# The low parts of every fourth weight chunk by an accumulating DMA, in a two-layer encoder in fp32

## The chip, the core and the metric

The kernel runs on one core of a Trainium2 chip. The engines that matter here are TensorE (matrix products), VectorE and ScalarE (elementwise work), GpSimd (hardly used before) and SyncE, from whose queue most transfers are issued. In the profile they are called PE (PEld for its weight loads), DVE, ACT, POOL and SP; a "q" behind the name is the engine's instruction queue where it issues a DMA. The metric is the device time of the whole kernel in microseconds.

## What is computed

The reference is an encoder of two layers on 256 tokens of width 2048, all in fp32. Each layer has a mixer (an mLSTM group, a retention group and a multi-head latent attention group, whose outputs are joined) and a feed-forward block:

```python
for l in range(DEPTH):                                   # DEPTH = 2
    h = _rms(x, g_mix[l])
    x = x + _mixer(h, cos, sin, w_in[l], ..., w_out[l])
    u = _rms(x, g_ffn[l])
    x = x + jnp.square(jax.nn.relu(u @ w_ff1[l])) @ w_ff2[l]     # 2048 -> 8192 -> 2048
return _rms(x, g_final)
```

Nearly all the arithmetic is products of the 256 tokens with weights: w_in (2048 x 4432), w_out (2048 x 2048), w_ff1 and w_ff2 (2048 x 8192 each way), and the smaller up-projections of the attention group.

## The kernel before

**Three products for one.** TensorE takes operands in a format (fp32r) that carries fewer bits than fp32 and goes through the array in one pass. The kernel therefore splits each operand into a high part, which is the value rounded to that format, and a low part, which is the rest. A product of two fp32 matrices becomes high x high, high x low and low x high.

**The stream of weights.** All weights lie in one flat array in the order of their use, cut into 737 chunks of 128 partitions x up to 1024 columns (512 KB). `weight_plan` writes that order down. The class `Stream` carries it out:

- `load` issues the DMA of a chunk from SyncE's queue into a tile `wraw`. There are NRAW = 4 buffers.
- `prep` makes the parts of a chunk: ScalarE copies `wraw` into `whi` (line 237), which rounds it, and VectorE writes `wlo = wraw - whi` (line 238). Then it asks for the load of the chunk four further on, for which a raw buffer must be free.
- `get(i)`, called when the products of chunk i are put down, first calls `prep` up to chunk i + 2. There are NHL = 4 buffers each of `whi` and `wlo`.

**The order of work.** The program is written straight out, and each engine executes its own list in that order; semaphores order the engines among each other. So the split of chunk i stands on ScalarE's list at the point where the products of chunk i - 2 begin, behind everything that was put down before that point. In the feed-forward part this matters: the blocks alternate between ff1 (four chunks, two tiles of hidden units, `ff_tile`) and ff2 (four chunks, one block of 512 output columns, `nat`). When a hidden tile is complete, `ff_evac` squares its positive part and splits it, with ScalarE's copy `fr` (line 1051), two VectorE operations, ScalarE's `hhi` (line 322) and VectorE's `hlo`. ScalarE's `fr` waits until TensorE has finished the tile. The first chunk split behind the second tile's evacuation is the third chunk of the ff2 block that follows.

**Which chunks the number falls on.** Chunks 0 to 112 of layer 0 are the mixer's; from 113 on the blocks of the feed-forward part begin at an index with remainder 1 when divided by 4. Layer 1 begins at chunk 369 and its feed-forward part at 481, again with remainder 1. So in the feed-forward parts the chunks with i % 4 == 3 are the third chunks of their blocks (for the very first ff1 block, the chunks are ordered otherwise, the third of the four as well). Of the 64 ff2 blocks of the two layers 56 follow an ff1 block and 8 follow another ff2 block.

**SyncE's queue** is in order: a load that waits for a raw buffer holds up every load behind it.

Of the kernel before, what the change touches and what calls it, by code (L numbers as in the profile page):

```python
# [18 lines left out]
P = 128  # L19
# [15 lines left out]

# columns of the constant array
C_MASK = 0
# [3 lines left out]
C_W = 816  # L41
# columns of a layer's parameter array
G_MIX, G_FFN, G_ML, G_RET, G_Q, G_KV, W_CONV, B_GATE, PAR_W = 0, 16, 32, 36, 40, 44, 46, 70, 86


# [1 line left out]
def weight_plan():  # L47
    """Blocks of weights in the order of their use; each is cut into chunks (k rows of tiles, columns)."""
    plan = []

    def nat(key, l, mat, kts, c0, w):
        per = max(1, CH // w)
        if not plan:
            kts0, kts = kts[:2], kts[2:]
            chunks = [([k], c0, w) for k in kts0]
        else:
            chunks = []
        chunks += [(kts[i:i + per], c0, w) for i in range(0, len(kts), per)]
        plan.append((key, l, mat, chunks))

    def stat(key, l, mat, kts, tiles):
        """One chunk per group of (tile, k) pairs, tile major."""
        per = CH // P
        pairs = [(t, k) for t in tiles for k in kts]
        chunks = [pairs[i:i + per] for i in range(0, len(pairs), per)]
        plan.append((key, l, mat, chunks))

    k16 = list(range(16))
    kout = [8, 9, 10, 11, 12, 13, 14, 15, 0, 1, 2, 3, 4, 5, 6, 7]
    for l in range(DEPTH):  # L70
        nat("c_q", l, "w_in", k16, 1024, 512)
        nat("c_kv", l, "w_in", k16, 1536, 336)
        nat("r_qk", l, "w_in", k16, 1872, 512)
        for h in range(0, 8, 4):
            stat(("kn", h), l, "w_kv_up", [0, 1], [h, h + 1, h + 2, h + 3])
        for b in range(2):
            nat(("v", b), l, "w_kv_up", [0, 1], 1024 + 512 * b, 512)
        for h in range(0, 8, 2):
            stat(("qn", h), l, "w_q_up", [0, 1, 2, 3], [h, h + 1])
        nat("qr", l, "w_q_up", [0, 1, 2, 3], 1024, 512)  # L80
        stat("ml_q", l, "w_in", k16, [0, 1, 2, 3])
        stat("ml_k", l, "w_in", k16, [4, 5, 6, 7])
        nat("ml_v", l, "w_in", k16, 2384, 512)
        nat("r_v", l, "w_in", k16, 2896, 512)
        nat("ml_o", l, "w_in", k16, 3408, 512)
        nat("r_g", l, "w_in", k16, 3920, 512)
        for part, kk in (("a", kout[:8]), ("b", kout[8:])):
            for b in range(2):
                nat(("out" + part, b), l, "w_out", kk, 512 * b, 512)
        for b in range(2, 4):  # L90
            nat(("out", b), l, "w_out", kout, 512 * b, 512)

        def ff1(g, i):
            f = g * 8 + 2 * i
            if g == 0 and i == 0:
                for half in range(2):
                    for t in range(2):
                        stat(("ff1", f + t, half), l, "w_ff1", k16[8 * half:8 * half + 8], [f + t])
            else:
                stat(("ff1", f), l, "w_ff1", k16, [f, f + 1])  # L100

        def ff2(g, b):
            nat(("ff2", g, b), l, "w_ff2", [g * 8 + i for i in range(8)], 512 * b, 512)

        for i in range(4):
            ff1(0, i)
        for g in range(NGRP):
            for i in range(4):
                if g + 1 < NGRP:
                    ff1(g + 1, i)  # L110
                ff2(g, i)
    return plan
# [8 lines left out]
def in_columns():  # L121
    """The columns of w_in in the order in which the blocks read them."""
    r = np.arange
# [85 lines left out]
class Stream:  # L209
    """The weights, chunk after chunk: read, then split into two parts that one pass carries exactly."""  # L210

# [17 lines left out]
    def prep(self, upto):  # L229
        while self.nprep < min(upto, len(self.sizes)):  # L230
# [6 lines left out]
            self.nc.scalar.activation(hi[:, :f], raw[:, :f], AF.Copy)  # L237
            self.nc.vector.tensor_tensor(lo[:, :f], raw[:, :f], hi[:, :f].bitcast(F32), op=ALU.subtract)  # L238
            self.parts[i] = (hi, lo)
# [10 lines left out]
def encoder_kernel(ctx: ExitStack, tc: tile.TileContext, xin, posin, w, par, const, gfin, out, dump=None):  # L250
# [13 lines left out]

# [1 line left out]
    cst = one.tile([P, C_W], F32, name="cst")  # L266
# [22 lines left out]

    # the clock of the tensor engine rises with use: products of zeros until the data is there  # L290
    warm = sp.tile([P, 512], mybir.dt.bfloat16, name="warm", tag="junk", bufs=1)
# [4 lines left out]

# [1 line left out]
    def bank(name):  # L298
# [6 lines left out]
    def rsqrt(dst, src, n, scale):  # L305
        """dst = 1 / sqrt(src * scale + EPS) on [P, n] by Newton's iteration, in steps."""
        nt = sp.tile([P, 3, n], F32, name="nt", tag=f"nt{n}", bufs=2 if n == 2 else 1)
# [11 lines left out]
    def split(*items):  # L319
        """hi + lo = src (* g) of each item, both in the one-pass format."""  # L320
        for hi, lo, src, *g in items:
# [12 lines left out]

# [1 line left out]
    side = []  # L336
    now = [0.0]

    class Task:
        """Steps of side work; a step yields the time to leave before the next one."""  # L340

# [43 lines left out]

# [1 line left out]
    chunk_no = [0]  # L387

    def nat_steps(chunks, ps, lh, ll, base, first, last):
        """ps[t] += (lh + ll)[k].T @ weights for both tiles of tokens."""  # L390
        n = sum(len(c[0]) for c in chunks)
# [21 lines left out]
    def stat(chunks, kts, rh, rl, dst):  # L413
        """dst[tile] = weights.T @ (rh + rl) for one tile of weight columns after another."""
        for c in chunks:
# [25 lines left out]
    def make_xT(b, g0, l, wait):  # L441
        """Columns 512 b .. of x, transposed and times the gain; their sums of squares."""
        for pr in range(2):
# [27 lines left out]
    def new_xT(b, g0, l, square, wait=0.8):  # L471
        """Starts the transposes of block b; after the last, the scale of the tokens."""
        xt_task[b] = add(make_xT(b, g0, l, wait), [(xt_task[b - 1], 2)] if b else [])
# [45 lines left out]
    def rope(dst, src, t, n):  # L519
        """Rotates n heads of 64: src [P, n * 64], dst that or [P, n, 64], of tile t of the tokens."""  # L520
        t1 = sp.tile([P, 512], F32, name="rp1", tag="rp1", bufs=1)[:, :n * 64]
# [15 lines left out]
    def layer(l):  # L537
        g = prm[:, l, :]
        L = {}

# [1 line left out]
        def ev_cq(ps):  # L542
# [60 lines left out]

# [1 line left out]
        def qr_task():  # L605
            qr = L["qr"]
            qd = ap.tile([P, 2, 8, 2, 64], F32, name="qd", tag="hlo", bufs=2)
            for t in range(2):
# [3 lines left out]
                yield 1.2  # L612
            # of each head the first part on 64 partitions, the second on the other 64
            qrT = L["qrT"] = ap.tile([P, 8, S], F32R, name="qrT", tag="hhi", bufs=2)
# [49 lines left out]

# [1 line left out]
        def gate_task():  # L666
# [31 lines left out]

            # lf <= 0, so that the running sum is never above its last term
            for d in range(2):  # L700
# [38 lines left out]

# [1 line left out]
        def ev_qk(i, pr, ps):  # L741
# [24 lines left out]

# [1 line left out]
        def ev_mlv(ps):  # L768
# [8 lines left out]
        def ml_head(h):  # L777
# [4 lines left out]
            hb, hs = L["hy"][:, 0], L["hs"]  # L782
            # blocks (direction, keys, queries): F00 F01 B10 B11 B00 F11
            wt = sp.tile([P, 768], F32, name="wt", tag="pr")
# [56 lines left out]
        def head_out(src, stat_, gate, k0, g0):  # L841
            """Normalises the heads in src, gates them and puts them at rows k0 .. of y transposed."""
            yhi, ylo = y0()
# [17 lines left out]

# [1 line left out]
        def ev_rqk(ps):  # L863
# [69 lines left out]

# [1 line left out]
        it = iter([p for p in plan if p[1] == l])  # L935
# [102 lines left out]

# [1 line left out]
        hts = {}  # L1040

        def ff_evac(f, ps):
            """The square of the positive part of tile f, split."""
            gi, i = divmod(f, 8)
# [11 lines left out]
        def ff_tile(ps, chunk, first, last):  # L1056
            """ps = [hi.T x + lo.T x's first part | hi.T x's second part]."""
            hi, lo = ws.get(chunk_no[0])
# [55 lines left out]

# [1 line left out]
    fin = {}  # L1116
# [13 lines left out]
    def last_block(chunks, lh, ll):  # L1130
        """The last columns, one tile of tokens after the other, each followed by its norm."""
        parts = []
# [82 lines left out]
```

## Time and profile before

| | us |
|---|---|
| median of 2 runs | 2184.4 |
| lowest and highest run | 2184.02, 2184.79 |
| span of the profiled execution | 2183.1 |
| TensorE products of a weight chunk with hidden units or xT in ff1 (f <- xT, whi and wlo) | 712.0 + 552.1 busy |
| ScalarE busy | 1044.0 |
| VectorE busy | 1354.7 |
| GpSimd busy | 0.2 |

The profile is of one execution. Its span is the time from the first to the last instruction, and the runs' times are a little longer than that. Busy times of an engine's instructions overlap where they are pipelined; TensorE's above all, so its groups add up to more than its busy time. A row of the timeline gives the start, the duration, the engine, the line, the operation with the tiles that it writes and reads, a count of instructions run together, and in brackets the idle time before it with what ended it.

### The profile page before, as it was taken

The page shows a single profiled execution, that of the slowest core. Times are in us where ns is not written, and L with a number is a line of the kernel's source. Part 1 is how long each engine was busy: PE and PEld are TensorE (multiplying, and loading weights), DVE is VectorE, ACT ScalarE, POOL GpSimd, SP SyncE. Part 2 cuts the span into 40 slices and gives each one's busy share as a digit, 9 for nine tenths or more (in the row PEclk, how much of TensorE's full clock was granted, in tenths as well). Part 3 has the DMA queues.
Part 4 walks back from the last instruction along what each step waited for, and adds up shares of the span by engine and source line. Part 5 has one row for each costly group of instructions (what it writes and reads, how often), then busy time and mean ns, then how long its engine had stood idle before and what let it go on. Part 6 is the DMA issues. An engine that isn't in the chain of part 4 may idle for free.

```text
span 2183.1 us, 29259 instructions
## 1 busy us (share of the span) xinstructions
PE 2164.9 (99%) x11280; PEld 1840.8 (84%) x11280; DVE 1354.7 (62%) x2019; ACT 1044.0 (48%) x1530; POOL 0.2 (0%) x4
## 2 busy tenths in 40 slices
PE   8999999999999999999999999999999999999998
PEld 7898888888888888888888978888888888888887
DVE  5667565666565656566666575756656565656655
ACT  5645655444444444444556455545444444444444
POOL 0000000000000000000000000000000000000000
PEclk9999999999999999999999999999999999999999
DMA  7544555566555556565565354555555555656554
GB/s 217 186 135 134 165 163 186 172 193 197 188 194 191 194 186 200 181 201 180 189 181 173 118 165 133 167 190 183 196 189 194 188 197 184 202 178 207 175 204 162
DMA packets 111356, 395.20 MB, mean 181 GB/s; under 512 B 12904, under 2 KB 14056, under 8 KB 111088
## 3 DMA queue, kind: packets, MB, share of 16 engines
q1 hardware_dynamic: 109072, 389.90, 54.7%
q10 hardware_dynamic: 2144, 3.43, 0.5%
q8 instruction: 88, 1.44, 0.3%
q14 instruction: 52, 0.43, 0.1%
HBM read 391.17 MB, written 2.12 MB: 180 GB/s over the span
## 4 chain that ended last, share of the span: by engine, by line
PE 95%; DVE 2%; ACT 1%; DMA 1%; issue 1%; ACTq 0%; SPq 0%; DVEq 0%
PE pm L333 57%; PE f L333 33%; PE sc L333 1%; DMA wraw<-in_w_dram 1%; DVE wlo L238 1%; PE o L333 1%; ACT whi L237 1%; PE ry L333 1%; PE num L333 0%; PE xt L330 0%; PE pt L330 0%; PE st L333 0%; ACT junk L303 0%; PE rs L333 0%; DVE mqk L765 0%
## 5 line engine op out<-in xcount | busy, mean ns | idle before, releaser
L238 DVE TENSOR_TENSOR wlo<-wraw,whi 128x1024 fp32r<-128x1024 f32 (+2 forms) x737 | 875.1, 1217 | 275.9 <-ACT whi L237 274.3
L237 ACT ACTIVATE whi<-wraw 128x1024 fp32r<-128x1024 f32 (+2 forms) x737 | 749.9, 1048 | 333.0 <-PE pm L333 286.6
L333 PE MATMUL f<-xT,whi 128*128 128x512 f32 x2048 | 712.0, 392 | 0.0
L333 PE MATMUL f<-xT,wlo 128*128 128x256 f32 x2048 | 552.1, 280 | 0.0
L333 PEld LDWEIGHTS f<-xT,whi 128*128 128x128 f32 x2048 | 379.4, 188 | 77.0
L333 PE MATMUL pm<-wlo,hhi 128*128 128x512 f32 (+1 forms) x1040 | 401.6, 386 | 0.6 <-DVE wlo L238 0.6
L333 PE MATMUL pm<-whi,hhi 128*128 128x512 f32 (+1 forms) x1040 | 402.1, 387 | 0.0
L333 PE MATMUL pm<-whi,hlo 128*128 128x512 f32 (+1 forms) x1040 | 401.2, 386 | 0.0
L333 PEld LDWEIGHTS f<-xT,wlo 128*128 128x128 f32 x2048 | 385.0, 188 | 11.3 <-DVE wlo L238 0.8
L333 PE MATMUL pm<-whi,xT 128*128 128x512 f32 (+1 forms) x896 | 291.3, 394 | 2.4 <-ACT whi L237 1.4
L333 PEld LDWEIGHTS pm<-wlo,hhi 128*128 128x128 f32 x1040 | 195.4, 188 | 40.2 <-DVE wlo L238 1.0
L333 PEld LDWEIGHTS pm<-whi,hlo 128*128 128x128 f32 x1040 | 195.4, 188 | 39.7
L1051 ACT ACTIVATE fr<-f 128x256 f32<-128x256 f32 x128 | 49.1, 384 | 374.3 <-PE f L333 374.3
L333 PEld LDWEIGHTS pm<-whi,hhi 128*128 128x128 f32 x1040 | 195.4, 188 | 37.2
L333 PEld LDWEIGHTS pm<-whi,xT 128*128 128x128 f32 x896 | 167.2, 189 | 37.5 <-ACT whi L237 1.6
L1052 DVE TENSOR_TENSOR fr<-f,fr 128x256 f32<-128x256 f32 x128 | 54.3, 424 | 218.0 <-ACT fr L1051 218.0
L1024 DVE SCALAR_TENSOR_TENSOR xx<-pm,rs,xx 128x512 f32<-128x512 f32 x126 | 90.1, 751 | 144.3 <-PE pm L333 144.3
L333 PE MATMUL pm<-wlo,xT 128*128 128x512 f32 (+1 forms) x448 | 173.5, 387 | 2.4 <-DVE wlo L238 2.3
L322 ACT ACTIVATE hhi<-fq 128x256 fp32r<-128x256 f32 x128 | 53.5, 418 | 126.8 <-DVE fq L1053 126.8
L333 PE MATMUL pm<-whi,yhi 128*128 128x512 f32 x256 | 101.5, 397 | 0.0
L333 PEld LDWEIGHTS pm<-wlo,xT 128*128 128x128 f32 x448 | 84.9, 189 | 19.6 <-DVE wlo L238 4.9
L333 PE MATMUL pm<-whi,ylo 128*128 128x512 f32 x256 | 99.8, 390 | 0.0
(235 smaller groups left out, 1614.7 us busy)
## 6 DMA issues: line engine op xcount, KB each, us to landing
wraw<-in_w_dram SPq DMA_DIRECT2D x723, 512.0 KB, 4.2
wraw<-in_w_dram SPq DMA_DIRECT2D x10, 504.0 KB, 6.7
wt<-mx_rows ACTq DMA_DIRECT2D x8, 256.0 KB, 3.7
out_dram<-xx SPq DMA_DIRECT2D x8, 256.0 KB, 3.3
xx<-in_x_dram SPq DMA_DIRECT2D x3, 512.0 KB, 8.1
gf<-in_gfin_dram ACTq DMA_DIRECT2D x1, 1024.0 KB, 6.1
xx<-in_x_dram SPq DMA_DIRECT2D x2, 256.0 KB, 3.8
wraw<-in_w_dram SPq DMA_DIRECT2D x2, 256.0 KB, 4.5
```

What stands on the lines that cost most here:

```text
L237: self.nc.scalar.activation(hi[:, :f], raw[:, :f], AF.Copy)
L238: self.nc.vector.tensor_tensor(lo[:, :f], raw[:, :f], hi[:, :f].bitcast(F32), op=ALU.subtract)
L322: A.activation(hi, src, AF.Copy, **({"scale": g[0]} if g else {}))
L333: T.matmul(ps, lhsT=lhsT, rhs=rhs, start=start, stop=stop)
L1024: V.scalar_tensor_tensor(x[t][:, xs], ps[t], scale[:, t:t + 1], x[t][:, xs], op0=ALU.mult, op1=ALU.add)
L1051: A.activation(r, ps[:, S:], AF.Copy)
L1052: V.tensor_tensor(r, ps[:, :S], r, op=ALU.add)
```

## The change

For every chunk i with i % 4 == 3 the subtraction on VectorE is left out. ScalarE makes the negative of the high part in the tile of the low part, by a second copy of the raw chunk with a scale of -1 (its output has the same rounded format), and a DMA issued from GpSimd's queue adds the raw chunk into that tile. The sum in the tile is the low part. The other chunks are as they were. Comments and docstrings of the file are dropped as well.

```diff
             self.nc.scalar.activation(hi[:, :f], raw[:, :f], AF.Copy)
-            self.nc.vector.tensor_tensor(lo[:, :f], raw[:, :f], hi[:, :f].bitcast(F32), op=ALU.subtract)
+            if i % 4 == 3:
+                self.nc.scalar.activation(lo[:, :f], raw[:, :f], AF.Copy, scale=-1.0)
+                self.nc.gpsimd.dma_start(out=lo[:, :f], in_=raw[:, :f], accum_op=ALU.add)
+            else:
+                self.nc.vector.tensor_tensor(lo[:, :f], raw[:, :f], hi[:, :f].bitcast(F32), op=ALU.subtract)
             self.parts[i] = (hi, lo)
```

That is 184 of the 737 chunks. Two queues show where the new instructions and waits come to stand, at the same place of layer 0: chunks 237 to 240 are an ff2 block, chunks 241 to 244 the ff1 block behind it. The number behind a tile's name is the chunk, the one behind the underscore counts tiles and differs between the programs.

ScalarE's list before, from the split of chunk 237 to the evacuation of the next ff1 block's first tile:

```order
L237 ACTIVATE whi237_6411<-wraw237_6324 128x1024
L237 ACTIVATE whi238_6433<-wraw238_6342 128x1024
L1051 ACTIVATE fr_6455<-f_6410 128x256
L322 ACTIVATE hhi_6221<-fq_6456 128x256
L237 ACTIVATE whi239_6464<-wraw239_6363 128x1024
L237 ACTIVATE whi240_6482<-wraw240_6385 128x1024
L237 ACTIVATE whi241_6500<-wraw241_6415 128x1024
L237 ACTIVATE whi242_6518<-wraw242_6437 128x1024
L237 ACTIVATE whi243_6539<-wraw243_6468 128x1024
L237 ACTIVATE whi244_6561<-wraw244_6486 128x1024
```

and after:

```order
L237 ACTIVATE whi237_6470<-wraw237_6382 128x1024
L237 ACTIVATE whi238_6492<-wraw238_6400 128x1024
L1055 ACTIVATE fr_6514<-f_6469 128x256
L326 ACTIVATE hhi_6278<-fq_6515 128x256
L237 ACTIVATE whi239_6523<-wraw239_6422 128x1024
L239 ACTIVATE wlo239_6524<-wraw239_6422 128x1024
L237 ACTIVATE whi240_6542<-wraw240_6444 128x1024
L237 ACTIVATE whi241_6560<-wraw241_6474 128x1024
L237 ACTIVATE whi242_6578<-wraw242_6496 128x1024
L237 ACTIVATE whi243_6599<-wraw243_6528 128x1024
L239 ACTIVATE wlo243_6600<-wraw243_6528 128x1024
L237 ACTIVATE whi244_6622<-wraw244_6546 128x1024
```

The splits keep their places; behind the high parts of chunks 239 and 243 there is now the negated copy into `wlo`. GpSimd's list has one DMA for each of them and nothing between.

SyncE's list before, the loads of chunks 243 to 249, with the semaphores that each waits for (DVE: VectorE is done with the buffer's last content; DMAHW: a transfer from an engine's queue):

```order
L224 DMA wraw243_6468<-in_w_dram 128x1024 [waits DMAHW6_49,DVE_49]
L224 DMA wraw244_6486<-in_w_dram 128x1024 [waits DMAHW7_49,DVE_49]
L224 DMA wraw245_6504<-in_w_dram 128x1024 [waits DMAHW0_49,DVE_49]
L224 DMA wraw246_6522<-in_w_dram 128x1024 [waits DMAHW1_49,DVE_49]
L224 DMA wraw247_6543<-in_w_dram 128x1024 [waits DMAHW2_49,DVE_49]
L224 DMA wraw248_6565<-in_w_dram 128x1024 [waits DMAHW3_49,DVE_49]
L224 DMA wraw249_6595<-in_w_dram 128x1024 [waits DMAHW4_49,DVE_49]
```

and after (DMASW: an accumulating transfer from GpSimd's queue; they use the semaphores DMASW0 to DMASW7 in turn, chunk 239's is DMASW3 and chunk 243's is DMASW4):

```order
L224 DMA wraw243_6528<-in_w_dram 128x1024 [waits DMAHW7_49,DVE_49]
L224 DMA wraw244_6546<-in_w_dram 128x1024 [waits DMAHW0_49,DVE_49]
L224 DMA wraw245_6564<-in_w_dram 128x1024 [waits DMAHW6_49,DMASW3_49]
L224 DMA wraw246_6582<-in_w_dram 128x1024 [waits DMAHW1_49,DVE_49]
L224 DMA wraw247_6604<-in_w_dram 128x1024 [waits DMAHW3_49,DVE_49]
L224 DMA wraw248_6626<-in_w_dram 128x1024 [waits DMAHW2_49,DMASW4_49]
L224 DMA wraw249_6656<-in_w_dram 128x1024 [waits DMAHW4_49,DVE_49]
```

The loads of chunks 245 and 248 now wait for the transfers of chunks 239 and 243, whose raw buffers they take over; the loads between them still wait for VectorE.

## The prediction

> **What bounds the kernel now.** First the busy shares and the DMA queues on the page, then the groups of its dearest lines.
>
> ```profile
> PE 2164.9 (99%) x11280; PEld 1840.8 (84%) x11280; DVE 1354.7 (62%) x2019; ACT 1044.0 (48%) x1530; POOL 0.2 (0%) x4
> ...
> q1 hardware_dynamic: 109072, 389.90, 54.7%
> ...
> L238 DVE TENSOR_TENSOR wlo<-wraw,whi 128x1024 fp32r<-128x1024 f32 (+2 forms) x737 | 875.1, 1217 | 275.9 <-ACT whi L237 274.3
> L237 ACT ACTIVATE whi<-wraw 128x1024 fp32r<-128x1024 f32 (+2 forms) x737 | 749.9, 1048 | 333.0 <-PE pm L333 286.6
> ```
>
> TensorE is busy in 99% of a span of 2183.1 us. VectorE is at 62% and ScalarE at 48%, so work taken from VectorE shortens nothing unless TensorE waited for it. The view of waits, TensorE's own and its weight loads', says how much that is:
>
> ```profile
> PE pm L333 <- DVE wlo L238: 4.4, 9, 0.9
> PE pm L333 <- ACT whi L237: 1.4, 1, 1.4
> PEld pm L333 <- DVE wlo L238: 8.3, 12, 1.1
> ```
>
> All waiting for low parts comes to 4.4 + 8.3 = 12.7 us, 0.6% of the span. A quarter of the chunks changes, so some 3 us is the most that the removed subtractions can give. What matters is how early a low part is ready now, and how much later it will be. For that I read the timeline of one feed-forward block, ScalarE first, then TensorE at the third chunk (whi239) of the ff2 block that follows an ff1 block:
>
> ```profile
> 729.00 0.38 ACT L1051 ACTIVATE fr<-f 128x256 f32<-128x256 f32 x1 [1.91 <-PE f L333]
> 730.33 0.42 ACT L322 ACTIVATE hhi<-fq 128x256 fp32r<-128x256 f32 x1 [0.95 <-DVE fq L1053]
> 730.65 2.94 ACT L237 ACTIVATE whi<-wraw 128x1024 fp32r<-128x1024 f32 x3
> 737.17 1.06 ACT L237 ACTIVATE whi<-wraw 128x1024 fp32r<-128x1024 f32 x1 [1.61 <-PE pm L333]
> ...
> 734.25 0.39 PE L333 MATMUL pm<-whi,hhi 128*128 128x512 f32 x1
> 734.48 0.39 PE L333 MATMUL pm<-wlo,hhi 128*128 128x512 f32 x1
> ...
> 745.48 0.28 PE L333 MATMUL f<-xT,wlo 128*128 128x256 f32 x1
> ```
>
> The reader is to see that the split of chunk 239 cannot start before the last ff1 tile has been evacuated (fr waits for TensorE until 729.00, hhi ends at 730.75), and that TensorE wants its low part at 734.48, under 4 us later. The third chunk of the next ff1 block (243) is split at 737.17 and wanted only at 745.48.
>
> **The change part by part.** *Removed:* 184 of the 737 subtractions (every i with i % 4 == 3), 184 x 1.217 = 224 us of VectorE, beside TensorE's work: at most the 3 us above.
>
> *Added on ScalarE:* 184 copies with scale -1 of the shape of the whi copies, 184 x 1.048 = 193 us, 48% to 57% busy: hidden, except that each stands ahead of its transfer and so counts in that chunk's chain. The whi copies behind it come 1.05 us later; they are of chunks that TensorE reaches at least a chunk later.
>
> *Added on GpSimd's queue:* 184 accumulating transfers of 512 KB from raw to low part. GpSimd has 4 small instructions now, so nothing is queued ahead of them but the previous transfer.
>
> *Waits.* TensorE's first product with wlo now waits for the transfer, and every later product is queued behind it. With L the time from the end of the negated copy to that product's release, the stall is L less the margin that the chunk has today.
>
> Margin of the ff2 chunk: three whi copies from 730.65, 1.05 each, so the first ends at 731.70; the negated copy ends at 732.75; wanted at 734.48: 1.73 us. There are 56 such chunks (28 ff2 blocks in each layer follow an ff1 block, one third chunk each). Margin of the ff1 chunk: 737.17 + 1.06 + 1.05 = 739.28, wanted at 745.48: 6.2 us; 54 of these. The other 74 I bound by a tight and a loose one of the out projection, the first of the two whi copies of 295.14 ending at 296.19:
>
> ```profile
> 295.14 2.00 ACT L237 ACTIVATE whi<-wraw 128x1024 fp32r<-128x1024 f32 x2
> 300.04 0.39 PE L333 MATMUL pm<-wlo,yhi 128*128 128x512 f32 x1
> ...
> 338.13 1.06 ACT L237 ACTIVATE whi<-wraw 128x1024 fp32r<-128x1024 f32 x1 [0.41 <-PE pm L333]
> 347.24 0.39 PE L333 MATMUL pm<-wlo,yhi 128*128 128x512 f32 x1
> ```
>
> 300.04 - 296.19 - 1.05 = 2.8 us, and 347.24 - 339.19 - 1.05 = 7.0 us; I take half of the 74 at each.
>
> *The unknown, L.* No transfer of this kind is in the trace. The nearest row is a plain load of the same 512 KB (the view of tile wraw):
>
> ```profile
> DMA to landing us min/median/max: 3.1/4.2/12.0
> ```
>
> Of this, the queue row above gives the moving: 54.7% of 2183.1 us over 737 loads is 1.62 us. The rest, 1.5 (minimum) to 2.6 us (median), is fixed. An accumulating transfer reads two tiles for one that it writes: two passes are 3.24 us, and L = 4.7 to 5.8. I take 5.5, in the upper half, since the descriptors come from another engine's queue. Lower end: one pass in the quickest load's time, 3.1. Upper end: three passes (4.86) with the slow fixed part (2.6), plus half of a load running beside it (0.8): 8.3.
>
> The Trainium skill, "DMA: Bandwidth & Descriptors", section "Anatomy of one DMA — SWDGE (gpsimd) path", fits a transfer issued by GpSimd as 2.0 us plus its bytes at 436 GB/s; for 512 KB I estimate from it 3.2 us, and 4.4 us if the bytes count twice. By 4.4 the sum below would be 2460 us. No run here shows it yet.
>
> *The clock.* A stall costs more than itself if the clock falls. The trace has one case, around 48 us (stage, length, busy time of each engine, granted clock, DMA share, GB/s):
>
> ```profile
> 47.00:50.00 3.00, 0.98 (x4) 0.75 (x5) 1.47 (x3) 2.87 (x5) 0.00 (x0) 1.00 0.89 330
> 50.00:52.00 2.00, 2.00 (x12) 2.00 (x11) 1.78 (x11) 2.00 (x3) 0.00 (x0) 0.68 0.71 233
> 52.00:54.00 2.00, 2.00 (x9) 2.00 (x8) 1.91 (x5) 0.13 (x1) 0.00 (x0) 0.50 0.63 182
> 54.00:56.00 2.00, 2.00 (x11) 1.76 (x10) 1.83 (x4) 1.57 (x5) 0.00 (x0) 0.97 0.58 199
> ```
>
> TensorE idled for 2.0 of 3 us, and the clock then stood at 0.5 for some 3.4 us, which loses 1.7 us of work. A stall of 3.8 us I charge 1.6 us, one of 2.7 us 1.0, one under 1.5 us nothing (estimates from these rows).
>
> The Trainium skill, "TensorE: Matmul & The Clock Gate", Part 1, lets the clock fall after at least one idle window of about 3.4 us. The trace differs, since 2 us of idling inside 3 us were enough; by the rule most stalls would cost no clock, and the sum would be about 2490 us.
>
> *Sum for L = 5.5:*
> - 56 ff2 chunks: 56 x (5.5 - 1.73) = 211
> - their clock: 56 x 1.6 = 90
> - 54 ff1 chunks: 5.5 is below 6.2: 0
> - 74 others: half x (2.7 + 1.0), half nothing: 74 x 1.85 = 137
> - subtractions removed: -3
>
> Together +435: 2183.1 + 435 = 2618 us of span. The medians of the runs lie 1.3 us above the span (2184.4), so 2620 us.
>
> *SP's queue.* Four chunks' loads in flight share four raw buffers, and one buffer is now held until its transfer lands. As the queue is ordered, the load behind the transfer of chunk 239 is that of chunk 245, and two loads stand behind it. Chunk 245 is used six chunks after 239. Two successive ff1 blocks (x64, 11.12 us) start 22.01 us apart with eight chunks between them, so a chunk takes 2.75 us and the load has some 16 us for its 4.2: I cost it at nothing, under cover of these six chunks.
>
> ```profile
> 717.84 11.12 PE f L333 x64
> ...
> 739.85 11.12 PE f L333 x64
> ```
>
> **The rivals.** *(a) The transfer is hidden and nothing changes.* If both sides being on chip made it quick, L could come near the ff2 margin. For: GpSimd's queue is empty, and no load is held up there. Against: the quickest plain load takes 3.1 us, with half the reading. It decides at L = 2.55, where 56 x 0.82 - 3 = 43 us is 2% of 2184.4; at L = 2.3 the time is 2183 + 32 - 3 + 1 = 2213 us. *(b) Slower, but little:* L between 2.55 and 3.1, for 2230 to 2270 us; it needs one pass and the best fixed part at once. *(c) The adding is the bound:* the transfer works far below copying speed, say L = 12 us. Then the ff1 chunks stall too: 56 x (10.3 + 1.7) + 54 x 5.8 + 74 x 8.8 (half at 9.2, half at 5.0, plus 1.7) = 672 + 313 + 651, so about 3820 us. For it speaks only that no row bounds the rate of adding; against it that the forecast already counts a second pass. Above L = 8.3 this is the case.
>
> The Trainium skill, "Collectives: The Full Stack", section "The bandwidth ceiling: the fold count and why AG ≠ RS ≠ AR", ascribes the halved rate of reducing transfers to the two reads and not to the adding, which speaks against (c); no run here shows that yet.
>
> **How the numbers follow.** Chance of the forecast (L from 3.1 to 8.3) 80%; (a) 4%, (b) 5%, (c) 11%. Lower end, L = 3.1: 56 x 1.37 = 77, others 74 x 0.15 = 11, less 3: 2270 us. Upper end, L = 8.3: 56 x (6.57 + 1.7) = 463, 54 x 2.1 = 113, others 74 x (3.4 + 0.85) = 315, less 3: 888, so 3070 us. The range is 2270 to 3070 and leaves 20% out, (a) and (b) below and (c) above. Within 2%, about what a measurement of this kernel can tell from no change, only (a) ends: 4%. Faster by 2% would need 44 us where 12.7 us is all the waiting for low parts: 1%, for what I overlook. Slower: 95%.
>
> **What would show it.** Right: TensorE's largest new wait is pm behind the transfer into wlo, some 3 to 4 us each at the third chunk of ff2 blocks, 56 times and nearly equal; ff1 chunks wait little; the transfer's time to landing is 4.5 to 6 us; the granted clock falls below 1.0 all through the feed-forward part; ScalarE gains some 190 us and VectorE loses some 220. Wrong: loads of wraw become what ScalarE waits for (then the held buffer counts, not L); the clock stays at 1.0 (then -127 us); or L lies outside 3.1 to 8.3.

## The result and the profile after

The changed kernel takes 2591.9 us (median of 2 runs, 2589.27 to 2594.53) against 2184.4 us: 1.187 times as long, with a 95% interval of 1.1845 to 1.1890. The profiled execution has a span of 2587.5 us, 404.4 us more than before. The forecast was 2620 us.

First the page of the changed kernel: busy shares, DMA queues (packets, MB, share of 16 engines), and the chain of work that ended last, by engine.

```profile
PE 2301.1 (89%) x11280; PEld 1917.9 (74%) x11280; DVE 1148.5 (44%) x1835; ACT 1213.7 (47%) x1714; POOL 158.9 (6%) x188
...
q1 hardware_dynamic: 109072, 389.90, 43.6%
q0 software_dynamic: 26496, 96.46, 20.9%
...
PE 72%; DMA 20%; ACT 5%; issue 2%; DVE 1%; SPq 0%; ACTq 0%; POOLq 0%
```

TensorE went from 99% to 89% of a longer span, and a fifth of the chain is now DMA. The same 11280 products are busy for 136 us more (2301.1 against 2164.9), and the time in which TensorE does nothing grew by 268 us (286.4 against 18.2). These two make up the 404 us. The groups of the page that were edited, and the products that use the result:

```profile
L237 ACT ACTIVATE whi<-wraw 128x1024 fp32r<-128x1024 f32 (+2 forms) x737 | 754.5, 1047 | 520.8 <-PE pm L337 494.3
L242 DVE TENSOR_TENSOR wlo<-wraw,whi 128x1024 fp32r<-128x1024 f32 (+2 forms) x553 | 657.6, 1218 | 426.1 <-ACT whi L237 424.8
...
L337 PE MATMUL pm<-wlo,hhi 128*128 128x512 f32 (+1 forms) x1040 | 443.9, 427 | 183.9 <-DMA wlo<-wraw 183.9
...
L240 POOL DMA_DIRECT2D wlo<-wraw x184 | 158.7, 862 | 2403.3 <-ACT wlo L239 1989.4
...
L239 ACT ACTIVATE wlo<-wraw 128x1024 fp32r<-128x1024 f32 x184 | 192.1, 1044 | 0.0
```

VectorE did give up its 184 subtractions (1354.7 us busy before, 1148.5 now). ScalarE and GpSimd were not short of time. But ahead of the ff2 products with low parts TensorE idles for 183.9 us, and what ends it is the transfer into `wlo`. The view of waits gives the whole of it (total, times, longest):

```profile
PEld pm L337 <- DMA wlo<-wraw: 281.4, 92, 4.8
PE pm L337 <- DMA wlo<-wraw: 245.0, 87, 4.4
...
PE f L337 <- DMA wlo<-wraw: 28.3, 10, 4.8
ACT whi L237 <- DMA wraw<-in_w_dram: 24.7, 12, 4.1
```

The product waits come to 245.0 + 28.3 = 273 us, which is the idle growth and a little more, since some short waits of before are gone (weight loads wait at the same moments and are not added). The last row is as important: loads of the raw chunks are what ScalarE waits for in only 24.7 us (39.2 before), so in this kernel the held raw buffer is not the trouble.

One such place in the timeline, the third chunk of an ff2 block behind an ff1 block; ScalarE, then TensorE, then GpSimd:

```profile
877.30 1.04 ACT L237 ACTIVATE whi<-wraw 128x1024 fp32r<-128x1024 f32 x1
878.25 1.04 ACT L239 ACTIVATE wlo<-wraw 128x1024 fp32r<-128x1024 f32 x1
...
880.89 0.39 PE L337 MATMUL pm<-whi,hhi 128*128 128x512 f32 x1
884.48 0.50 PE L337 MATMUL pm<-wlo,hhi 128*128 128x512 f32 x1 [3.20 <-DMA wlo<-wraw]
...
879.58 0.87 POOL L240 DMA_DIRECT2D wlo<-wraw  x1 [14.39 <-ACT wlo L239]
```

The negated copy ends at 879.29, GpSimd begins the issue 0.29 us later and is at it for 0.87 us, and TensorE, which starts a product every 0.23 us here and so wanted the low part at 881.12, gets it at 884.48. L, from the end of the negated copy to that product, is 5.19 us. Over all 56 places of this kind the trace's records give a mean of 5.20 (5.13 to 5.55) and an idle time of 3.2 us each, 180 us together. The 54 third chunks of ff1 blocks behind ff2 blocks idle for 0.6 us together; the 74 others for 93 us.

Most of the 136 us more of busy time, 122 us by the mean granted clocks (0.951 against 0.998), are the clock. An estimate for the rest: a product ahead of a wait counts as busy for 0.39 us, where otherwise the next one begins after 0.23 us, and 0.16 us at 97 waits are 16 us. The view of windows around this stall and the next ff2 stall (stretch, length, busy time of PE, PEld, DVE, ACT and POOL, granted clock, DMA share, GB/s):

```profile
881.00:884.00 3.00, 0.28 (x2) 0.00 (x0) 2.76 (x3) 1.20 (x2) 0.00 (x0) 1.00 1.06 190
884.00:887.00 3.00, 2.52 (x11) 2.10 (x12) 0.00 (x0) 0.00 (x0) 0.00 (x0) 1.00 1.00 389
...
906.00:909.00 3.00, 0.79 (x4) 0.33 (x2) 3.00 (x3) 1.70 (x2) 0.00 (x0) 1.00 1.01 175
909.00:912.00 3.00, 1.99 (x5) 1.61 (x6) 0.27 (x1) 0.00 (x0) 0.00 (x0) 0.66 0.90 356
912.00:915.00 3.00, 3.00 (x12) 2.40 (x11) 0.00 (x0) 0.55 (x1) 0.00 (x0) 0.77 0.87 339
915.00:918.00 3.00, 3.00 (x17) 2.52 (x16) 1.43 (x2) 2.31 (x3) 0.86 (x1) 1.00 0.01 4
```

Of two nearly equal stalls, the one released at 884.48 leaves the clock at 1.0, and the one released at 910.01 is followed by half clock: (1 - 0.66) x 3 + (1 - 0.77) x 3 = 1.7 us of work lost, that is 3.4 us at half speed. Read in the same way in the 5 us behind each of the 56 releases, the clock falls in 51 of them and 87 us are lost. The other five have none.

### The profile page after: what moved, and what is told of

It reads as the page before. It is cut to its first block, busy times and chain, and to the rows that moved or that the text cites. A ratio compares the mean times of both kernels' runs of the same rounds, so it can differ in the third digit from the quotient of the medians.

```text
span 2587.5 us, 29629 instructions
## 1 busy us (share of the span) xinstructions
PE 2301.1 (89%) x11280; PEld 1917.9 (74%) x11280; DVE 1148.5 (44%) x1835; ACT 1213.7 (47%) x1714; POOL 158.9 (6%) x188
## 3 DMA queue, kind: packets, MB, share of 16 engines
q0 software_dynamic: 26496, 96.46, 20.9%
## 4 chain that ended last, share of the span: by engine, by line
PE 72%; DMA 20%; ACT 5%; issue 2%; DVE 1%; SPq 0%; ACTq 0%; POOLq 0%
PE pm L337 42%; PE f L337 26%; DMA wlo<-wraw 19%; ACT wlo L239 3%; ACT whi L237 1%; PE sc L337 1%; DMA wraw<-in_w_dram 1%; PE o L337 1%; PE ry L337 0%; PE xt L334 0%; PE num L337 0%; PE pt L334 0%; PE st L337 0%; ACT junk L307 0%; DVE fq L1057 0%
## 5 line engine op out<-in xcount | busy, mean ns | idle before, releaser
L242 DVE TENSOR_TENSOR wlo<-wraw,whi 128x1024 fp32r<-128x1024 f32 (+2 forms) x553 | 657.6, 1218 | 426.1 <-ACT whi L237 424.8
L337 PE MATMUL pm<-wlo,hhi 128*128 128x512 f32 (+1 forms) x1040 | 443.9, 427 | 183.9 <-DMA wlo<-wraw 183.9
L337 PE MATMUL f<-xT,wlo 128*128 128x256 f32 x2048 | 557.7, 282 | 28.3 <-DMA wlo<-wraw 28.3
L337 PE MATMUL pm<-whi,hlo 128*128 128x512 f32 (+1 forms) x1040 | 435.6, 419 | 0.0
L337 PE MATMUL pm<-whi,hhi 128*128 128x512 f32 (+1 forms) x1040 | 435.6, 419 | 0.0
L337 PEld LDWEIGHTS pm<-wlo,hhi 128*128 128x128 f32 x1040 | 216.3, 208 | 253.5 <-DMA wlo<-wraw 208.2
L240 POOL DMA_DIRECT2D wlo<-wraw x184 | 158.7, 862 | 2403.3 <-ACT wlo L239 1989.4
L337 PEld LDWEIGHTS pm<-whi,hlo 128*128 128x128 f32 x1040 | 216.8, 209 | 45.7
L337 PEld LDWEIGHTS pm<-whi,hhi 128*128 128x128 f32 x1040 | 216.4, 208 | 46.2
L239 ACT ACTIVATE wlo<-wraw 128x1024 fp32r<-128x1024 f32 x184 | 192.1, 1044 | 0.0
L337 PE MATMUL pm<-wlo,yhi 128*128 128x512 f32 x256 | 102.0, 399 | 14.3 <-DMA wlo<-wraw 14.1
```

The source lines that it names most:

```text
L239: self.nc.scalar.activation(lo[:, :f], raw[:, :f], AF.Copy, scale=-1.0)
L240: self.nc.gpsimd.dma_start(out=lo[:, :f], in_=raw[:, :f], accum_op=ALU.add)
L337: T.matmul(ps, lhsT=lhsT, rhs=rhs, start=start, stop=stop)
```

## The experiments

Each diff is against the changed kernel unless it says otherwise. Ratios are to the kernel before (2184 us), timed on the same chip with the run.

### The two new pieces, each off the path to TensorE

e1_neg_only keeps the negated copy and lets VectorE write the low part over it; there is no transfer.

```diff
             if i % 4 == 3:
                 self.nc.scalar.activation(lo[:, :f], raw[:, :f], AF.Copy, scale=-1.0)
-                self.nc.gpsimd.dma_start(out=lo[:, :f], in_=raw[:, :f], accum_op=ALU.add)
-            else:
-                self.nc.vector.tensor_tensor(lo[:, :f], raw[:, :f], hi[:, :f].bitcast(F32), op=ALU.subtract)
+            self.nc.vector.tensor_tensor(lo[:, :f], raw[:, :f], hi[:, :f].bitcast(F32), op=ALU.subtract)
```

> The 184 negated copies on ScalarE alone, written into wlo and then overwritten by VectorE's subtraction; no transfer. Theory (the cost is the transfer's delay beyond the margin, and the clock that falls after the stall): 2184 to 2195 us, since a subtraction that starts 1.05 us later still ends before TensorE wants it. Rival A (ScalarE's additional copies hold up its other work): at least 2280 us, a quarter of the +407.

e2_dma_beside makes copy and transfer for the 128 chunks of the feed-forward parts, but into a spare tile that nobody reads, while VectorE makes the low part.

```diff
-            if i % 4 == 3:
-                self.nc.scalar.activation(lo[:, :f], raw[:, :f], AF.Copy, scale=-1.0)
-                self.nc.gpsimd.dma_start(out=lo[:, :f], in_=raw[:, :f], accum_op=ALU.add)
-            else:
-                self.nc.vector.tensor_tensor(lo[:, :f], raw[:, :f], hi[:, :f].bitcast(F32), op=ALU.subtract)
+            if i in self.some:
+                spare = self.spare.tile([P, CH], F32R, name=f"wsp{i}", tag="nat", bufs=2)
+                self.nc.scalar.activation(spare[:, :f], raw[:, :f], AF.Copy, scale=-1.0)
+                self.nc.gpsimd.dma_start(out=spare[:, :f], in_=raw[:, :f], accum_op=ALU.add)
+            self.nc.vector.tensor_tensor(lo[:, :f], raw[:, :f], hi[:, :f].bitcast(F32), op=ALU.subtract)
```

> In the feed-forward parts (128 chunks) the negated copy and the accumulating transfer go to a spare tile that nobody reads, and VectorE makes every low part as before; the mixer is as before. Theory: 2184 to 2205 us, since TensorE waits for no transfer. Rival B (the transfers' traffic delays the loads of weights or the engines): 2300 us or more, and waits of ScalarE for wraw grow.

Measured: e1 2192.7 us, ratio 1.0038 (1.0024 to 1.0053); e2 2189.7 us, ratio 1.0026 (1.0017 to 1.0035). ScalarE's extra 170 us cost at most 8 us. The transfers with their DMA traffic, GpSimd's queue and the raw buffer held until landing, for 128 of the 184 chunks, cost 5. One sign of rival B did appear in e2: ScalarE's waits for loads grew from 39.2 us to 262.1.

```profile
ACT whi L239 <- DMA wraw<-in_w_dram: 262.1, 70, 7.1
```

Loads do come later here, but TensorE hardly notices. Whether the held buffer or the traffic delays them, e2 doesn't separate. So the added work is nearly hidden, and nearly the whole loss comes from TensorE's dependence on the transfer's end. The 8 us of e1 are more than the "hidden" that I had costed. In 3.4 of them TensorE's products wait longer for VectorE's low parts (7.8 us against 4.4), which belongs to the experiment, where the subtraction comes behind the negated copy; the others are not settled.

### Which chunks it is

e5_ff1_only and e6_ff2_only apply the change to one kind of chunk each and leave the rest as before; the list `some` holds the 54 third chunks of ff1 blocks behind ff2 blocks, or the 56 of ff2 blocks behind ff1 blocks.

```diff
+        keys = [(k, n) for k, _, _, cs in plan for n in range(len(cs))]
+        self.some = [i for i, (k, n) in enumerate(keys) if i % 4 == 3 and k[0] == "ff2" and keys[i - 4][0][0] == "ff1"]
...
-            if i % 4 == 3:
+            if i in self.some:
```

> The change only in the third chunks of the 54 ff1 blocks that follow an ff2 block (margin 6.2 us). Theory: 2184 to 2190 us, no stall. Rival D (each transfer costs about the same wherever it stands): 54/184 of +407, so 2300 us.

> The change only in the third chunks of the 56 ff2 blocks that follow an ff1 block (margin 1.7 us). Theory: 56 x 3.4 us of stall and 56 x 1.6 us of clock, 2465 us (2440 to 2490). Rival D: 56/184 of +407, so 2308 us.

Measured: e5 2186.1 us, ratio 1.0008 (0.9999 to 1.0018); e6 2464.0 us, ratio 1.128 (1.1258 to 1.1303). The waits of e6:

```profile
PEld pm L339 <- DMA wlo<-wraw: 204.3, 56, 4.1
PE pm L339 <- DMA wlo<-wraw: 180.7, 56, 3.7
```

56 transfers, 56 waits, 3.2 us each. The same transfer costs nothing where the low part is due more than 6 us behind the negated copy, and 280 / 56 = 5.0 us of time where it is due under 2 us behind it. Of the 407.5 us, 279.8 belong to the ff2 chunks, 1.9 to the ff1 chunks, and what remains if the parts simply add up, 126 us, to the other 74.

### What the latency is made of

e3_plain_copy takes the adding away, so that the transfer is a plain copy of the same 512 KB (these low parts are then not the right ones); e4_half adds, but only half of the columns, and VectorE subtracts the others.

```diff
-                self.nc.gpsimd.dma_start(out=lo[:, :f], in_=raw[:, :f], accum_op=ALU.add)
+                self.nc.gpsimd.dma_start(out=lo[:, :f], in_=raw[:, :f])
```

```diff
-                self.nc.scalar.activation(lo[:, :f], raw[:, :f], AF.Copy, scale=-1.0)
-                self.nc.gpsimd.dma_start(out=lo[:, :f], in_=raw[:, :f], accum_op=ALU.add)
+                self.nc.scalar.activation(lo[:, :f // 2], raw[:, :f // 2], AF.Copy, scale=-1.0)
+                m = f // 2
+                self.nc.gpsimd.dma_start(out=lo[:, :m], in_=raw[:, :m], accum_op=ALU.add)
+                self.nc.vector.tensor_tensor(lo[:, m:f], raw[:, m:f], hi[:, m:f].bitcast(F32), op=ALU.subtract)
```

> The transfer as a plain copy of the raw chunk, without the adding (the low part of these chunks is then the weight itself). Theory with the second pass as part of the delay: the transfer is some 1.4 us shorter (2.94 us of moving now against 1.53 for a load), so the ff2 stall falls from 3.4 to 2.0 us and the time to 2360 to 2460 us. Rival C (what counts is the issue and completion on GpSimd's queue, whatever is moved): 2550 us or more.

> Only the first half of each fourth chunk's columns by the transfer, the second half by VectorE. Theory: half of 2.94 us of moving saved, so as for the plain copy 2360 to 2460 us. Rival C: 2550 us or more, since as many rows of half the length are issued.

Measured: e3 2317.3 us, ratio 1.0609 (1.0588 to 1.0631); e4 2312.8 us, ratio 1.0589 (1.0568 to 1.0610). Both came out below what I had expected. The views of tile `wlo`, of the changed kernel, of e3 and of e4 (GpSimd's issue: ns min/median/max; then us from issue to landing):

```profile
L240 POOL DMA_DIRECT2D wlo<-wraw x184: 859/859/1002, 16.3 to 2561.6; - x184
...
DMA to landing us min/median/max: 4.5/4.8/10.2
```

```profile
L240 POOL DMA_DIRECT2D wlo<-wraw x184: 527/527/662, 16.1 to 2294.1; - x184
...
DMA to landing us min/median/max: 2.8/3.1/10.4
```

```profile
L241 POOL DMA_DIRECT2D wlo<-wraw x184: 859/859/1002, 15.3 to 2287.9; - x184
...
DMA to landing us min/median/max: 3.2/3.4/9.7
```

And the queue of GpSimd's transfers on the page of e3, then of e4:

```profile
q0 software_dynamic: 26496, 96.46, 11.6%
```

```profile
q0 software_dynamic: 26496, 48.24, 12.0%
```

The moving takes 20.9% of 2587.5 us over 184 transfers, 2.94 us, with the adding; 11.6% of 2315.6, 1.46 us, without; and 12.0% of 2312.3, 1.51 us, for half the bytes with the adding. Adding thus doubles the moving, and halving the bytes halves it. GpSimd's issue depends on the adding (0.86 against 0.53 us) and not on the bytes. With that, L at the ff2 chunks is 5.20 us in the changed kernel and 3.22 in e3: 1.5 of the 2 us between them are moving and 0.3 the issue.

The Trainium skill, "Collectives: The Full Stack", section "The bandwidth ceiling: the fold count and why AG ≠ RS ≠ AR", puts the halved rate of reducing transfers down to their two reads; the factor of 2.0 between 2.94 and 1.46 us agrees, though these runs do not tell a second read from any other cost that is proportional to the bytes.

Two things made both runs faster than expected. The ff2 stalls are 1.2 us each and not the 2.0 that I had expected, since I had started from 3.4 us instead of 3.2 and taken off 1.4 us alone. And stalls of this length leave the granted clock at 1.0 behind all 56 releases, in e3 as in e4; the mean clocks are 0.993 and 0.994.

### The clock by itself

e9_filled puts 14 products whose result nobody uses ahead of the third chunk of the ff2 blocks that follow an ff1 block (`fill` is set for these), so that TensorE works while it waits. L is not touched.

```diff
+            if fill and chunk_no[0] % 4 == 3:
+                idle = bank("idle")
+                for _ in range(14):
+                    mm(idle, lh(kts[0])[:, :P], hi[:, :512])
```

> As the changed kernel, with 14 products into a bank that nobody reads (3.2 us) ahead of the third chunk of the 56 ff2 blocks, so that TensorE works while it would wait 3.4 us. Theory with the clock: the stalls cost as much as before, but the clock stays at 1.0 there, and some 90 us go: 2480 to 2520 us. Rival E (the clock has no part in it): 2590 us or more.

Measured: 2517.5 us, ratio 1.1525 (1.1502 to 1.1548), 74 us below the changed kernel. The windows of e9 around one such place, the 14 products running from 868.98 for 3.34 us:

```profile
866.00:870.00 4.00, 4.00 (x19) 3.30 (x18) 1.65 (x2) 4.00 (x5) 0.87 (x1) 1.00 0.46 132
870.00:874.00 4.00, 3.98 (x18) 2.98 (x17) 1.85 (x2) 0.29 (x1) 0.00 (x0) 1.00 1.02 278
874.00:878.00 4.00, 4.00 (x19) 3.29 (x19) 0.57 (x1) 2.01 (x2) 0.26 (x1) 1.00 0.85 322
```

TensorE is busy throughout and the clock stays at 1.0. The mean clock of the run rises from 0.951 to 0.982. Doing useless work in the wait is faster than idling through it, so the loss that I read from the windows is real time and not an effect of how the clock is recorded: 74 us came back of the 87.

### Moving the need, and moving the source

e8_hi_first puts a chunk's products with the high parts first, so that in an ff2 chunk 8 products instead of 1 stand ahead of the first that needs the low part.

```diff
                     mm(ps[t][:, :cw], ha[:, tk], whi, st, False)
-                    mm(ps[t][:, :cw], ha[:, tk], wlo, False, False)
-                    mm(ps[t][:, :cw], la[:, tk], whi, False, en)
+                    mm(ps[t][:, :cw], la[:, tk], whi, False, False)
+                    late.append((t, ha[:, tk], wlo, en))
...
+            for t, h, wlo, en in late:
+                mm(ps[t][:, :cw], h, wlo, False, en)
```

> As the changed kernel, but in the blocks of natural order all products with whi of a chunk stand ahead of those with wlo, so wlo is wanted 7 to 8 products of 0.227 us (1.7 us) later. Theory: the ff2 stall falls from 3.4 to 1.7 us, the clock mostly holds, and the time is 2340 to 2420 us. Rival (the stall is set by something else than the time at which wlo is wanted): 2550 us or more.

Measured: 2386.2 us, ratio 1.0924 (1.0903 to 1.0946). L is the same (5.21 us by the records), and the idle time at the 56 places falls from 3.2 to 1.63 us, by 7 products of 0.23 us. Only one of the 56 stalls is now followed by a fall of the clock, whose mean is 0.986.

e12_before_hi_first makes the same edit in the kernel before, to see whether the order is worth something by itself.

> The kernel before, with only the order of products turned round in the blocks of natural order: of each chunk those with whi ahead of those with wlo. Low parts are then wanted 0.2 to 1.7 us later, and most of the 12.7 us of waiting for them lies in such blocks at the start of a layer. Theory: 2174 to 2182 us, faster than both kernels. Rival (the waits pass on to the high parts or the loads): 2184 us.

Measured: 2187.1 us, ratio 1.0011 (1.0002 to 1.0020): no gain. The rival's case came: the products' waits for low parts fell from 4.4 us to 1.0, but those for a high part grew from 1.4 to 3.3, and ScalarE's for loads from 39.2 to 108.7. No version here is faster than the kernel before.

e7_early leaves the need and moves the source: every fourth chunk is split one chunk earlier, ahead of the last ff1 tile's evacuation. e10_early_half does the same with the change on every eighth chunk, which in the feed-forward parts are ff2 chunks, but for four in the first ff1 blocks.

```diff
-        self.prep(i + NHL - 1)
+        self.prep(i + NHL - 1 + ((i + NHL - 1) % 4 == 3))
```

```diff
-            if i % 4 == 3:
+            if i % 8 == 7:
...
-        self.prep(i + NHL - 1)
+        self.prep(i + NHL - 1 + ((i + NHL - 1) % 8 == 7))
```

> As the changed kernel, but a fourth chunk is split one chunk earlier in the program, ahead of the evacuation that holds up ScalarE. The ff2 margin grows from 1.7 to over 5 us, so those stalls go. In this order the load of chunk i + 4 waits for the transfer of chunk i, and the ring of load (4.4), two copies (2.1), and transfer (5.2) is 11.8 us against 11.0 us of products in four chunks. Theory: 0 to 0.8 us for each of the 184, 2200 to 2340 us. Rival (the margin is not what counts): 2500 us or more.

> As e7_early, but only every eighth chunk (i % 8 == 7, the ff2 blocks' among them) goes by the transfer, so that the ring has eight chunks' time. Theory: nearly every transfer is hidden, 2184 to 2225 us. Rival (a transfer costs some 2 us wherever it stands): 92 x 2.2 = +200, so 2385 us.

Measured: e7 2362.8 us, ratio 1.0811 (1.0789 to 1.0832), a little above the expected range; e10 2354.8 us, ratio 1.0787 (1.0760 to 1.0814), a clear miss. The margin did grow, to some 5.6 us, but L grew too: by the records to 7.26 us in e7 and 7.29 in e10, so that 1.4 and 1.6 us of stall are left at the 56 places. The view of tile `wlo` and the waits in e10:

```profile
DMA to landing us min/median/max: 4.5/6.8/10.0
```

```profile
ACT whi L237 <- DMA wraw<-in_w_dram: 266.4, 77, 6.4
...
PE pm L337 <- DMA wlo<-wraw: 119.1, 71, 3.7
```

The median landing is 2 us later than in the changed kernel, and ScalarE waits 266 us for loads, against 24.7. That second number doesn't explain the first: in e8 ScalarE waits 282 us for loads and L is 5.21. The windows from the end of the negated copy to the release, in the changed kernel and then in e10, show what else the DMA engines were doing:

```profile
879.29:881.00 1.71, 1.71 (x9) 1.31 (x7) 0.73 (x1) 1.71 (x2) 0.87 (x1) 1.00 0.00 0
881.00:883.00 2.00, 0.28 (x2) 0.00 (x0) 2.00 (x3) 1.20 (x2) 0.00 (x0) 1.00 1.10 209
883.00:884.48 1.48, 0.00 (x0) 0.00 (x1) 0.76 (x1) 0.00 (x0) 0.00 (x0) 1.00 1.03 221
```

```profile
865.84:867.00 1.16, 1.16 (x6) 0.94 (x6) 0.69 (x2) 0.39 (x2) 0.86 (x1) 1.00 0.85 307
867.00:869.00 2.00, 2.00 (x10) 1.66 (x9) 0.99 (x3) 1.74 (x3) 0.00 (x0) 1.00 1.01 254
869.00:871.00 2.00, 2.00 (x11) 1.65 (x10) 1.96 (x2) 0.70 (x1) 0.00 (x0) 1.00 1.04 242
871.00:873.07 2.07, 0.49 (x3) 0.07 (x2) 0.63 (x1) 1.06 (x1) 0.00 (x0) 1.00 0.33 63
```

In the changed kernel the DMA engines are idle (share 0.00) until the transfer starts, and move 209 x 2 + 221 x 1.48 = 745 KB until it lands. At the earlier place they are busy with loads from the start and move about 1480 KB before the product is released. Twice the bytes beside a longer transfer: this fits loads that share the engines with it. The packet records say the same. At the 56 places the transfer's first packet comes 2.28 us behind the start of the issue in e10 and 1.43 us in the changed kernel, and first and last packet are 4.43 us apart against 3.12, though the transfer's own packets keep the engines no longer busy (2.65 us against 3.05). And in e3, one kernel with one kind of transfer, the ff2 places, with almost no load beside them, land after 2.88 us, and the 54 ff1 places, with 757 KB of loads on average beside them, after 4.31.

e11_load_beside was to show that by itself: the changed kernel, with one further load of 512 KB, into a spare tile that nobody reads, issued from ScalarE's queue behind the negated copy of the 56 ff2 chunks.

```diff
+                if i in self.some:
+                    spare = self.spare.tile([P, CH], F32, name=f"wsp{i}", tag="nat", bufs=2)
+                    self.nc.scalar.dma_start(
+                        out=spare[:, :f], in_=self.w[self.offs[i]:self.offs[i + 1]].rearrange("(p f) -> p f", p=P))
```

> As the changed kernel, with one more load of 512 KB from ScalarE's queue into a tile that nobody reads, issued right behind the negated copy of the third chunk of the 56 ff2 blocks, so that it runs beside the transfer. Theory F (a transfer runs slower beside loads; in the kernel with the earlier split of every eighth chunk it took 7.3 us from the negated copy instead of 5.2): 1 to 2 us more stall at 56 places, 2640 to 2720 us. Rival (the longer transfer there has another cause, such as GpSimd's issue): 2590 to 2610 us.

Measured: 2570.9 us, ratio 1.1769 (1.1734 to 1.1803), which neither theory gives. The timeline tells why:

```profile
878.33 0.33 ACTq L245 DMA_DIRECT2D wsp<-in_w_dram  x1
878.54 1.04 ACT L239 ACTIVATE whi<-wraw 128x1024 fp32r<-128x1024 f32 x1
879.49 1.04 ACT L241 ACTIVATE wlo<-wraw 128x1024 fp32r<-128x1024 f32 x1
```

The load depends on neither copy. Its issue is on record before the two copies ran, 2.2 us ahead of the negated copy's end (880.53), and by the packet records all of it had been moved when the transfer's packets began, 1.7 us behind that end. The load ran ahead of the transfer and not beside it, so the run does not test the sharing. It shows the opposite case instead: no load's packet lies between the transfer's first and last, which are 2.77 us apart (in the changed kernel 82 KB do, and it is 3.12 us), and L is 4.93 us instead of 5.20. With stalls of 2.9 us the clock falls behind 42 of the 56 and not 51. So all that the traces hold points to the loads, but it is an observation: no run puts a load beside the transfer and changes nothing else.

## Why the prediction was right

The terms of the sum, forecast and measured:

| term | forecast, us | measured, us |
|---|---|---|
| L at the ff2 chunks | 5.5 | 5.20 |
| stalls of the 56 ff2 chunks | 211 | 180 |
| their clock | 90 | 87 |
| 54 ff1 chunks | 0 | 0.6 |
| stalls of the 74 others | 100 | 93 |
| clock of the whole | 127 | 122 |
| span | +435 | +404 |

The clock of the whole is worked out from the mean granted clock, 0.049 x 2587.5 - 0.002 x 2183.1. Stalls and clock come to 180 + 93 + 122 = 395 of the 404 us; the other 9 are not attributed.

- *What bounds the kernel, and what the removed subtractions give.* Right in saying that it is next to nothing, though the 12.7 us add weight loads to products that wait at the same moments: the products' waits for VectorE's low parts fell from 4.4 us to none in the view, and that is all that 206 us less of VectorE bought.
- *The added copies and issues are hidden.* Right to within 8 us of 2184 (e1), and within 5 for the transfers (e2).
- *The margins.* Right. 1.73 us was forecast at the ff2 chunk, and the row after has 881.12 - 879.29 = 1.83. That it is the margin that decides and not the number of transfers is shown by e5 and e6, which run the same transfer at 54 and 56 places for 2 and 280 us.
- *L.* Two passes and a fixed part was the right form. The moving, 2.94 us, is twice the plain 1.46 (e3), where I had taken twice a load's 1.62. The fixed part was 2.3 us, inside the 1.5 to 2.6 taken from loads, but made of other things: 0.29 us to the issue, 0.86 us of issue on GpSimd, and the rest mostly before the first and behind the last packet. I chose 5.5 in the upper half of 4.7 to 5.8; it was 5.2.
- *The clock.* The charge of 1.6 us for a stall of 3.8 us was taken from one case in the trace of before. It held in size (87 us against 90), but this nearness is partly luck: between the charges of 1.0 us at 2.7 and 1.6 us at 3.8, a stall of 3.2 us would have been charged 1.3 us, 71 us for the 56. A fall doesn't grow with its stall. At these places it costs 1.7 us or nothing, and what grows is how often it comes: behind none of 56 stalls of 1.2 us (e3, and e4), 1 and 4 of 56 of 1.6 us (e8, e10), 42 of 56 of 2.9 us (e11) and 51 of 56 of 3.2 us. "None under 1.5 us" is confirmed by e3; that the loss is real time, by e9.
- *The 74 others.* Right in size: 34 of them wait over 1 us, and all come to 93 us, where 37 waits of 2.7 us were forecast. That half of them would be like each of two places was taken without a reason, so here too there is luck.
- *SyncE's queue.* Right that it costs next to nothing: 5 us with the traffic (e2). SyncE now waits for transfers into `wlo` before reusing a raw buffer, 492.3 us in 183 waits, and in this kernel ScalarE's waits for loads nevertheless fell. That the loads always come in time is not shown: in e2 ScalarE waits 262 us for them and in e8 282, and what makes them late there is open.
- *The rivals.* A hidden transfer would have needed L near 2.5 us, and even the plain copy has 3.2 (e3). That the adding itself is the bound needed L above 8.3.
- *What is off.* The forecast lies 28 us above the time, and the mis-sized term is that of the ff2 stalls, 31 us too large: 56 x 0.3 = 17 us for L, 56 x 0.1 = 6 us for the margin, and 56 x 0.16 = 9 us from how idle time is counted, from the end of the product before, which lies 0.16 us behind the point where the next could have begun. The last is time all the same and belongs to the 9 us left unattributed. The range of 800 us was wide for what was known: its ends stood for L of 3.1 and 8.3 us, and the adding transfer in its own place came near neither.

Two rules of the Trainium skill had been weighed there. "DMA: Bandwidth & Descriptors", section "Anatomy of one DMA — SWDGE (gpsimd) path", led to estimates of 3.2 us for a plain transfer and 4.4 us with the bytes twice; the traces have 3.1 and 4.8 us from issue to landing, so it holds for the plain one and is 0.4 us short for the adding one, near the 0.33 us that its issue takes longer. "TensorE: Matmul & The Clock Gate", Part 1, asks for an idle window of about 3.4 us before the clock falls; here stalls of 3.2 us were followed by a fall in 51 of 56 cases, and the time they cost agrees with the trace's own case and not with the rule as it stands there; less than 3.4 us of idling was enough.

## What to carry to other kernels

Before handing a step to a slower but idle unit, read from the timeline how long after its input the result is wanted, place by place: the same transfer was free at 54 places with 6 us of margin and cost 5 us of time at each of 56 places with less than 2. Off-loading an engine that nobody waits for gave nothing here, though 206 us of its work disappeared. If a TensorE stall can't be avoided, keep it short (here 1.2 us cost no clock, and 3.2 us mostly cost another 1.7) or fill it with products.

## What was not expected of the hardware

- Of the 56 nearly equal stalls five were followed by no fall of the clock, and they don't stand at random. Half clock lasts some 3.4 us each time, but from one stall to the next it begins about 0.2 us later behind the release; after 8 to 16 stalls one has no fall, and the series starts again at the release. The windows of the changed kernel behind the release at 2386.59, late in such a series, show the fall a good microsecond after TensorE is back at work:

```profile
2386.59:2387.59 1.00, 1.00 (x4) 0.86 (x5) 0.00 (x0) 0.00 (x0) 0.00 (x0) 1.00 0.95 389
2387.59:2388.09 0.50, 0.50 (x3) 0.42 (x2) 0.00 (x0) 0.00 (x0) 0.00 (x0) 0.84 1.05 426
2388.09:2391.09 3.00, 3.00 (x8) 2.32 (x8) 0.00 (x0) 0.46 (x1) 0.00 (x0) 0.50 1.02 407
2391.09:2391.59 0.50, 0.50 (x3) 0.36 (x3) 0.00 (x0) 0.50 (x1) 0.00 (x0) 0.74 0.61 246
```

  The next stall, 3.17 us long like this one, has none, and the one behind that has its fall at once. The trace's own record of the clock shows the reason. All 66 falls of this run lie at whole multiples of 3.413 us from each other: the clock changes on a grid of its own, and stalls that come every 27.1 us drift against eight of its steps (27.3 us). What seems to decide is how long TensorE had no product within the step before. Behind every step at full clock with at least 1.90 us of that the clock fell, behind those with at most 1.87 us it never did; in e6 the border lies between 1.80 and 1.94 us, in e11 between 1.85 and 1.86. A stall of 3.2 us that an edge of the grid cuts into two parts below 1.9 us costs no clock. A few falls elsewhere come at less (1.38 us within the first 9 us of e10), so this is not the whole rule.
- GpSimd takes 0.86 us to issue an adding transfer and 0.53 us for a plain one of the same shape, and the same 0.86 us for half the columns.
- Issued with 3.7 us more margin, where loads are under way, the adding transfer lands after 6.8 us (median, e10) and not 4.8. Moving a transfer forward gained margin and lost more than half of it again.
